# A first load cut at partition 16, and one semaphore for the three sources of a last product (Poisson loss, one core)

## The chip, the cores and the metric

One core of one Trainium2 chip. The metric is device microseconds (us) of the run; a profile's span begins with the first DMA issue and is 1.3 to 1.5 us shorter.

## The reference

```python
def setup_inputs():
    batch, dim = 1024, 4096
    # log_input: randn, target: integers 0..9, both float32

def reference(log_input, target):
    loss = np.exp(log_input) - target * log_input
    return np.mean(loss, axis=-1).astype(np.float32)
```

Two inputs of 16 MiB are read once, and 4 KiB are written.

## The kernel before

Each partition takes eight consecutive rows of each input (128 KiB of it). SyncE issues all loads; ScalarE takes exponentials with row sums, VectorE products with row sums; the last row is cut into small loads, so that little is left to do when the last bytes land. The last product also adds up the partial sums of that row.

```python
    x_v = log_input.rearrange("(p b) d -> p (b d)", b=nb)
    ...
    early = []
    for i, (what, lo, w) in enumerate(loads):
        ...
        src = x_v if what == "x" else t_v
        dma = nc.sync.dma_start(out=place(what, lo, w), in_=src[:, lo : lo + w])
        dma.then_inc(landed[i], 16)
        if lo < 6 * d:
            early.append(dma.ins)
    before_first_barrier(nc, early)      # the first four loads go out ahead of the start barrier
    ...
    for j, (lo, w, i) in enumerate(t_work):
        ...
        nc.vector.wait_ge(landed[x_load], 16)
        if j < n_t - 1:
            ...   # product of (up to) one row: .wait_op(landed[i], 16).then_inc(prod_done, 1)
        else:
            nc.vector.wait_ge(ones_done, 1)
            nc.vector.wait_ge(landed[i], 16)
            nc.vector.wait_ge(prod_done, n_t - 1)
            nc.vector.tensor_tensor_reduce(
                ...   # the last 384 columns and the partial sums of the last row
            ).wait_op(exp_done, n_x, "sem-ge").then_inc(loss_done, 1)
```

Of the kernel before, what the change touches and what calls it, by code (L numbers as in the profile page):

```python
# [8 lines left out]


TAIL = [("x", 24), ("t", 12), ("t", 12), ("x", 6), ("t", 5), ("x", 2), ("t", 3)]


def before_first_barrier(nc, instructions):





    here, first = nc.cur_bb.bb, nc.main_func.blocks[0]  # L20
    names = {i.name for i in instructions}
    here.instructions = [i for i in here.instructions if i.name not in names]
    at = next(
        k
        for k, i in enumerate(first.instructions)
        if i.engine == mybir.EngineType.SP and i.opcode == "Drain"
    )
    first.instructions = first.instructions[:at] + instructions + first.instructions[at:]


def kernel(tc, log_input, target, out):














    nc = tc.nc
    tc.close()
    tc.compile()  # L48

    P = nc.NUM_PARTITIONS  # L50
    n, d = log_input.shape
    nb = n // P
    assert nb * P == n and tuple(target.shape) == (n, d) and nb == 8 and d % 32 == 0
    inv_d = 1.0 / d
    last_row = nb - 1

    x_v = log_input.rearrange("(p b) d -> p (b d)", b=nb)
    t_v = target.rearrange("(p b) d -> p (b d)", b=nb)
    out_v = out.rearrange("(p b) -> p b", b=nb)


    loads = []
    for first, rows in ((0, 4), (4, 2), (6, 1)):
        loads += [("x", first * d, rows * d), ("t", first * d, rows * d)]
    at = {"x": last_row * d, "t": last_row * d}
    for what, w in TAIL:
        loads.append((what, at[what], w * d // 32))
        at[what] += w * d // 32
    assert at == {"x": nb * d, "t": nb * d}


    def work(kind):
        todo = []
        for i, (what, lo, w) in enumerate(loads):
            if what == kind:
                step = min(w, d)
                todo += [(a, step, i) for a in range(lo, lo + w, step)]
        return todo

    x_work, t_work = work("x"), work("t")  # L80
    n_x, n_t = len(x_work), len(t_work)
    n_parts = n_x - last_row + n_t - last_row - 1

    big = {
        "x": nc.alloc_sbuf_tensor("x_big", [P, 4 * d + n_parts], F32).ap(),
        "t": nc.alloc_sbuf_tensor("t_big", [P, 4 * d + n_parts], F32).ap(),
    }
    mid = {
        "x": nc.alloc_sbuf_tensor("x_mid", [P, 2 * d], F32).ap(),
        "t": nc.alloc_sbuf_tensor("t_mid", [P, 2 * d], F32).ap(),  # L90
    }

    def place(what, lo, w):
        row = lo // d
        if 4 <= row < 6:
            return mid[what][:, lo - 4 * d : lo - 4 * d + w]
        if row >= 6:
            lo -= (6 if row == 6 else 4) * d
        return big[what][:, lo : lo + w]

    e_dump = nc.alloc_psum_tensor("e_dump", [P, d], F32).ap()

    parts = nc.alloc_sbuf_tensor("parts", [P, 2 * last_row], F32).ap()
    join_dump = nc.alloc_sbuf_tensor("join_dump", [P, 2 * last_row], F32).ap()
    all_loss = nc.alloc_sbuf_tensor("all_loss", [P, nb], F32).ap()

    def part(k):
        return big["t"][:, 4 * d + k : 4 * d + k + 1]

    landed = [nc.alloc_semaphore(f"landed{i}") for i in range(len(loads))]  # L110
    exp_done = nc.alloc_semaphore("exp_done")
    prod_done = nc.alloc_semaphore("prod_done")
    join_done = nc.alloc_semaphore("join_done")
    ones_done = nc.alloc_semaphore("ones_done")
    loss_done = nc.alloc_semaphore("loss_done")
    out_done = nc.alloc_semaphore("out_done")


    early = []
    for i, (what, lo, w) in enumerate(loads):  # L120
        if what == "x" and lo in (6 * d, 7 * d):
            free = 1 if lo == 6 * d else 4
            nc.sync.wait_ge(exp_done, free)
            nc.sync.wait_ge(prod_done, free)  # L124
        src = x_v if what == "x" else t_v
        dma = nc.sync.dma_start(out=place(what, lo, w), in_=src[:, lo : lo + w])  # L126
        dma.then_inc(landed[i], 16)
        if lo < 6 * d:
            early.append(dma.ins)
    before_first_barrier(nc, early)  # L130


    nc.gpsimd.memset(big["x"][:, 4 * d : 4 * d + n_parts], -1.0).then_inc(ones_done, 1)  # L133


    def join(row, exps):
        nc.scalar.wait_ge(exp_done, exps)
        nc.scalar.activation(  # L138
            out=join_dump[:, 2 * row : 2 * row + 2],
            in_=parts[:, 2 * row : 2 * row + 2],  # L140
            func=ACT_F.Copy,
            scale=inv_d,
            accum_out=all_loss[:, row : row + 1],
        ).wait_op(prod_done, row + 1, "sem-ge").then_inc(join_done, 1)

    for k, (lo, w, i) in enumerate(x_work):
        row, col = lo // d, lo % d
        if col == 0 and row >= 2:
            join(row - 2, k)
        elif col == 0 and row == 1:  # L150
            nc.scalar.wait_ge(exp_done, k)
        nc.scalar.activation(  # L152
            out=e_dump[:, col : col + w],
            in_=place("x", lo, w),
            func=ACT_F.Exp,
            bias=0.0,
            scale=1.0,
            accum_out=parts[:, 2 * row : 2 * row + 1] if row < last_row else part(k - last_row),
        ).wait_op(landed[i], 16, "sem-ge").then_inc(exp_done, 1)
        if col == 0 and row == last_row:  # L160
            join(row - 1, k + 1)


    for j, (lo, w, i) in enumerate(t_work):
        row = lo // d
        x_load = next(ix for a, wx, ix in x_work if a + wx >= lo + w)
        nc.vector.wait_ge(landed[x_load], 16)  # L167
        if j < n_t - 1:
            nc.vector.tensor_tensor_reduce(  # L169
                out=place("t", lo, w),  # L170
                in0=place("t", lo, w),
                in1=place("x", lo, w),
                scale=-1.0,
                scalar=0.0,
                op0=ALU.mult,
                op1=ALU.add,
                accum_out=parts[:, 2 * row + 1 : 2 * row + 2]
                if row < last_row
                else part(n_x - last_row + j - last_row),
            ).wait_op(landed[i], 16, "sem-ge").then_inc(prod_done, 1)  # L180
        else:
            nc.vector.wait_ge(ones_done, 1)
            nc.vector.wait_ge(landed[i], 16)  # L183
            nc.vector.wait_ge(prod_done, n_t - 1)  # L184
            nc.vector.tensor_tensor_reduce(  # L185
                out=place("t", lo, w + n_parts),
                in0=place("t", lo, w + n_parts),
                in1=place("x", lo, w + n_parts),
                scale=-inv_d,
                scalar=0.0,  # L190
                op0=ALU.mult,
                op1=ALU.add,
                accum_out=all_loss[:, last_row : last_row + 1],
            ).wait_op(exp_done, n_x, "sem-ge").then_inc(loss_done, 1)


    nc.sync.wait_ge(join_done, last_row)
    nc.sync.dma_start(out=out_v, in_=all_loss).wait_op(loss_done, 1, "sem-ge").then_inc(
        out_done, 16
    )  # L200
    used = landed + [exp_done, prod_done, join_done, ones_done, loss_done]
    nc.sync.sem_clear(range(used[0].num, out_done.num))
    assert all(used[0].num <= s.num < out_done.num for s in used)
    nc.sync.wait_ge(out_done, 16).then_inc(out_done, -16)
# [30 lines left out]
```

## Time and profile before

| | before |
|---|---|
| time | 84.22 us (84.13 to 84.23) |
| span of the profile | 82.7 us |
| first exponential starts (first load landed) | 21.73 us |
| first product starts (second load landed) | 41.07 us |
| last product starts | 80.67 us |
| store issued | 81.27 us |

The first two loads are 8 MiB each, so their landings give the rate of the stream and the lateness of its start. The lines (start, length, engine, line, output and inputs):

```profile
21.73 3.59 ACT L152 ACTIVATE e_dump<-x_big 128x4096 f32<-128x4096 f32 x1 [17.47 <-DMA x_big<-in_log_input_dram]
41.07 4.43 DVE L169 CUSTOM_DVE_ANT_0 t_big<-t_big,x_big 128x4096 f32<-128x4096 f32 x1 [41.07 <-DMA t_big<-in_target_dram]
```

The lines of the start and of the end are shown in the prediction.

### The profile page before, as it was taken

Reading aid. Unit: us, or ns where it says so; the run is one execution under the profiler, and the core shown is the slowest. Engines: PE = TensorE matmul, PEld = TensorE weight load, DVE = VectorE, ACT = ScalarE, POOL = GpSimd, SP = SyncE. Lnnn points to the kernel's source line nnn. Section 1 sums busy time; section 2 is a strip of 40 time slices with the busy share of each in tenths; the row PEclk is TensorE's granted clock in tenths of the full one; section 3 lists DMA queues with packets and bytes.
Section 4 is the critical chain, followed back from the end, with each engine's and each line's share of the span. In section 5 each row is a group of like instructions: output and inputs, shape, how many; then the busy total and the mean of one; then the engine's idle time right before and its main releaser. Section 6 shows DMA issues by size and latency. Waiting matters only on the chain.

```text
span 82.7 us, 136 instructions
## 1 busy us (share of the span) xinstructions
DVE 35.6 (43%) x22; ACT 33.2 (40%) x35; POOL 0.3 (0%) x5
## 2 busy tenths in 40 slices
DVE  0000000000000000000199999999379995994982
ACT  0500000000499910000000998979792595029360
POOL 0000000000000000000000000000000000000000
DMA  9199999919999991999599699799799999999960
GB/s 507 63 444 507 507 507 507 507 63 444 507 507 507 507 475 63 475 507 507 254 507 475 285 507 507 317 444 507 341 420 404 483 388 436 380 413 428 403 214 2
DMA packets 2016, 33.56 MB, mean 406 GB/s; under 512 B 352, under 2 KB 608, under 8 KB 1120
## 3 DMA queue, kind: packets, MB, share of 16 engines
q1 hardware_dynamic: 2016, 33.56, 95.6%
HBM read 33.55 MB, written 0.00 MB: 406 GB/s over the span
## 4 chain that ended last, share of the span: by engine, by line
DMA 72%; DVE 14%; issue 10%; SPq 2%; DVEq 0%
DMA t_big<-in_target_dram 72%; DVE t_big L169 13%; SPq L126 2%; DVE t_big L185 1%; DVE parts L169 0%; DVEq L184 0%; DVEq L183 0%; DVEq L167 0%; SPq L124 0%; DVE all_loss L185 0%
## 5 line engine op out<-in xcount | busy, mean ns | idle before, releaser
L169 DVE CUSTOM_DVE_ANT_0 t_big<-t_big,x_big 128x4096 f32<-128x4096 f32 (+2 forms) x8 | 26.2, 3308 | 43.4 <-DMA t_big<-in_target_dram 43.2
L152 ACT ACTIVATE e_dump<-x_big 128x4096 f32<-128x4096 f32 (+3 forms) x8 | 21.8, 2730 | 23.9 <-DMA x_big<-in_log_input_dram 23.6
L138 ACT ACTIVATE join_dump<-parts 128x2 f32<-128x2 f32 x7 | 1.4, 203 | 20.4 <-DVE parts L169 20.3
L169 DVE CUSTOM_DVE_ANT_0 t_mid<-t_mid,x_mid 128x4096 f32<-128x4096 f32 x2 | 8.8, 4422 | 2.0 <-DMA t_mid<-in_target_dram 2.0
L152 ACT ACTIVATE e_dump<-x_mid 128x4096 f32<-128x4096 f32 x2 | 7.1, 3568 | 0.0
L152 ACT ACT_TABLE_LOAD x1 | 1.3, 1283 | 3.0 <-PEq L48 3.0
L152 ACT ACTIVATION_READ_ACCUMULATOR e_dump<-x_big 128x1 f32 x8 | 1.5, 186 | 0.0
L138 ACT ACTIVATION_READ_ACCUMULATOR join_dump<-parts 128x1 f32 x7 | 1.3, 187 | 0.0
L185 DVE CUSTOM_DVE_ANT_0 t_big<-t_big,x_big 128x390 f32<-128x390 f32 x1 | 0.6, 568 | 0.2 <-ACT e_dump L152 0.2
L169 DVE DVE_READ_ACCUMULATOR2_ANT parts<- 128x1 f32 x7 | 0.6, 83 | 0.0
L152 ACT ACTIVATION_READ_ACCUMULATOR e_dump<-x_mid 128x1 f32 x2 | 0.4, 186 | 0.0
L169 DVE DVE_READ_ACCUMULATOR2_ANT t_big<- 128x1 f32 x3 | 0.3, 84 | 0.0
L133 POOL MEMSET x_big<- 128x6 f32 x1 | 0.1, 103 | 2.5 <-POOLq L48 2.5
L219 POOL MEMSET const-uint8-127<- 128x1 uint8 x1 | 0.1, 102 | 0.0
L219 POOL MEMSET const-bfloat16-1.0<- 128x1 bf16 x1 | 0.1, 101 | 0.0
L219 POOL MEMSET const-float32-0.0<- 128x1 f32 x1 | 0.1, 98 | 0.2 <-issue 0.2
L219 POOL MEMSET const-float32-1.0<- 128x1 f32 x1 | 0.1, 98 | 0.0
L185 DVE DVE_READ_ACCUMULATOR2_ANT all_loss<- 128x1 f32 x1 | 0.1, 85 | 0.0
## 6 DMA issues: line engine op xcount, KB each, us to landing
x_mid<-in_log_input_dram SPq DMA_DIRECT2D x1, 4096.0 KB, 49.9
t_mid<-in_target_dram SPq DMA_DIRECT2D x1, 4096.0 KB, 59.1
x_big<-in_log_input_dram SPq DMA_DIRECT2D x1, 2048.0 KB, 19.8
t_big<-in_target_dram SPq DMA_DIRECT2D x1, 2048.0 KB, 24.3
x_big<-in_log_input_dram SPq DMA_DIRECT2D x1, 1536.0 KB, 15.3
t_big<-in_target_dram SPq DMA_DIRECT2D x2, 768.0 KB, 17.5
x_big<-in_log_input_dram SPq DMA_DIRECT2D x1, 384.0 KB, 18.7
t_big<-in_target_dram SPq DMA_DIRECT2D x1, 320.0 KB, 19.1
```

Source lines behind the costliest of these rows:

```text
L126: dma = nc.sync.dma_start(out=place(what, lo, w), in_=src[:, lo : lo + w])
L133: nc.gpsimd.memset(big["x"][:, 4 * d : 4 * d + n_parts], -1.0).then_inc(ones_done, 1)
L138: nc.scalar.activation(out=join_dump[:, 2 * row : 2 * row + 2], in_=parts[:, 2 * row : 2 * row + 2], func=ACT_F.Copy, scale=inv_d, accum_o ...
L152: nc.scalar.activation(out=e_dump[:, col : col + w], in_=place("x", lo, w), func=ACT_F.Exp, bias=0.0, scale=1.0, accum_out=parts[:, 2 * ro ...
L169: nc.vector.tensor_tensor_reduce(out=place("t", lo, w), in0=place("t", lo, w), in1=place("x", lo, w), scale=-1.0, scalar=0.0, op0=ALU.mult ...
L185: nc.vector.tensor_tensor_reduce(out=place("t", lo, w + n_parts), in0=place("t", lo, w + n_parts), in1=place("x", lo, w + n_parts), scale= ...
L219: nc = _bacc.Bacc("TRN2", target_bir_lowering=False, num_devices=1)
```

## The change

The intent of the first part: the last product waits for three late sources. Where two of them are awaited by separate wait instructions, those run one after the other once the sources are in (0.05 us each, at 80.44 and 80.54 us in the chain of the kernel before); if all three count on one semaphore, which the product waits on itself, no wait instruction is left between the last source and the product. The intent of the second part: a first load of 16 partitions is one row for each of 16 DMA engines, so that all engines might begin sooner.

```diff
+FIRST = 16
-    landed = [nc.alloc_semaphore(f"landed{i}") for i in range(len(loads))]
+    landed = [nc.alloc_semaphore(f"landed{i}") for i in range(len(loads) - 1)]
+    full = [32] + [16] * (len(loads) - 2)
+    last_ready = nc.alloc_semaphore("last_ready")
...
-        dma = nc.sync.dma_start(out=place(what, lo, w), in_=src[:, lo : lo + w])
-        dma.then_inc(landed[i], 16)
+        cuts = [0, FIRST, P] if i == 0 else [0, P]
+        sem = landed[i] if i < len(loads) - 1 else last_ready
+        for a, b in zip(cuts, cuts[1:]):
+            dma = nc.sync.dma_start(out=place(what, lo, w)[a:b], in_=src[a:b, lo : lo + w])
+            dma.then_inc(sem, 16)
...
-        ).wait_op(landed[i], 16, "sem-ge").then_inc(exp_done, 1)
+        ).wait_op(landed[i], full[i], "sem-ge").then_inc(
+            exp_done if k < n_x - 1 else last_ready, 1
+        )
...
-        nc.vector.wait_ge(landed[x_load], 16)
+        if j == 0 or x_load > t_work[j - 1][2]:
+            nc.vector.wait_ge(landed[x_load], full[x_load])
...
-            ).wait_op(landed[i], 16, "sem-ge").then_inc(prod_done, 1)
+            ).wait_op(landed[i], full[i], "sem-ge").then_inc(
+                prod_done if j < n_t - 2 else last_ready, 1
+            )
         else:
             nc.vector.wait_ge(ones_done, 1)
-            nc.vector.wait_ge(landed[i], 16)
-            nc.vector.wait_ge(prod_done, n_t - 1)
+            nc.vector.wait_ge(exp_done, n_x - 1)
+            nc.vector.wait_ge(prod_done, n_t - 2)
...
-            ).wait_op(exp_done, n_x, "sem-ge").then_inc(loss_done, 1)
+            ).wait_op(last_ready, 18, "sem-ge").then_inc(loss_done, 1)
```

More of the change, by code (lines that the diff above doesn't have):

```diff
@@ L125 @@
         src = x_v if what == "x" else t_v
-        dma = nc.sync.dma_start(out=place(what, lo, w), in_=src[:, lo : lo + w])
-        dma.then_inc(landed[i], 16)
-        if lo < 6 * d:
-            early.append(dma.ins)
+        cuts = [0, FIRST, P] if i == 0 else [0, P]
[3 more added lines that the diff above has]
+            dma.then_inc(sem, 16)
+            if lo < 6 * d:
+                early.append(dma.ins)
     before_first_barrier(nc, early)
@@ L200 @@
     )
-    used = landed + [exp_done, prod_done, join_done, ones_done, loss_done]
+    used = landed + [last_ready, exp_done, prod_done, join_done, ones_done, loss_done]
     nc.sync.sem_clear(range(used[0].num, out_done.num))
```

## The prediction

> **What bounds the kernel now.** I read the page's busy shares and slices first, then the chain of work that ended last, then the timelines of both ends, then the DMA rates over short windows at the start. From the page:
>
> ```profile
> DVE 35.6 (43%) x22; ACT 33.2 (40%) x35; POOL 0.3 (0%) x5
> DMA  9199999919999991999599699799799999999960
> q1 hardware_dynamic: 2016, 33.56, 95.6%
> ```
>
> No engine is half busy; the DMA slices are full from the first to the last but one (a lone 1 is an effect of the record: a large packet is booked where it starts). The queue is busy for 95.6% of 82.7 us. So the kernel is one stream of 33.55 MB, and the span is the time until the stream runs, plus the stream, plus a tail after it. The stream's rate: the timeline starts the first exponential, which waits for the first load, at 21.73 us and the first product, which waits for the second load, at 41.07. Both loads are 8 MiB, so 8 MiB take 19.34 us: 434 GB/s, or 27.1 GB/s for each of 16 engines, and one row of 64 KiB takes an engine 2.42 us. The whole 32 MiB at that rate are 77.4 us of the 82.7. The end, in the chain:
>
> ```profile
> 60.46 19.11 DMA t_big<-in_target_dram
> 79.57 0.02 issue
> 79.60 0.83 DVE t_big L169 x2
> 80.43 0.01 issue
> 80.44 0.05 DVEq L183
> 80.49 0.05 issue
> 80.54 0.05 DVEq L184
> 80.59 0.09 issue
> 80.67 0.57 DVE t_big L185
> 81.24 0.01 DVE all_loss L185
> ```
>
> L183 and L184 are separate wait instructions ahead of the last product (L185); between the end of the previous product (80.43) and the start of the last there are 0.24 us of nothing but waits and their dispatch. The timeline says when the three sources were ready:
>
> ```profile
> 79.95 0.39 ACT L152 ACTIVATE e_dump<-x_big 128x256 f32<-128x256 f32 x1 [0.27 <-DMA x_big<-in_log_input_dram]
> 80.28 0.19 ACT L152 ACTIVATION_READ_ACCUMULATOR e_dump<-x_big 128x1 f32 x1
> 80.35 0.08 DVE L169 DVE_READ_ACCUMULATOR2_ANT t_big<- 128x1 f32 x1
> 80.67 0.57 DVE L185 CUSTOM_DVE_ANT_0 t_big<-t_big,x_big 128x390 f32<-128x390 f32 x1 [0.24 <-ACT e_dump L152]
> 81.27 0.35 SPq L198 DMA_DIRECT2D out_dram<-all_loss  x1
> ```
>
> The last exponential's sum is out at 80.28 + 0.19 = 80.47, the product before at 80.43. The third source, the last load, comes from the view of DMA issues: issued at 61.42 and 19.0 us to landing, so at about 80.42. All three come within 0.06 us of each other. The start, as engine rates in windows of 0.2 to 0.5 us (the last two columns are DMA share and GB/s):
>
> ```profile
> 0.50:1.00 0.50, 0.00 (x0) 0.00 (x0) 0.00 (x0) 1.00 0.39 131
> 1.00:1.20 0.20, 0.00 (x0) 0.00 (x0) 0.00 (x0) 1.00 11.02 3604
> 1.20:1.40 0.20, 0.00 (x0) 0.00 (x0) 0.00 (x0) 1.00 1.92 655
> 1.40:1.60 0.20, 0.00 (x0) 0.00 (x0) 0.00 (x0) 1.00 0.83 328
> 1.80:2.00 0.20, 0.00 (x0) 0.00 (x0) 0.00 (x0) 1.00 0.76 328
> ```
>
> Rate times window is the bytes of the packets that start in it; over 65,536 this gives 1, 11, 2, 1 and 1 packets: sixteen, one for each engine. The first engine starts 1.0 us after the first issue began, the last nearly 1 us later. The trace starts the second packets at 4.05 to 4.44 us; less 2.42 us, the engines are at full rate, in effect, only from 1.63 to 2.03 us on.
>
> [...]
>
> **The change, part by part.** (a) *The last product's waits.* The last load, the next-to-last product and the last exponential now raise one semaphore (16 + 1 + 1 = 18), and the product waits for it itself. What still stands ahead as wait instructions is met early: the exponentials but one by 79.69, the products but two by 79.54, the next-to-last load at 60.94 + 19.0 = 79.94. So those waits finish by about 80.1[...]. From semaphore to start is then one hop, as for the 640-wide product: landing at 79.57, start at 79.60, 0.02 us. New start: 80.47 + 0.02 = 80.49 or 80.50 instead of 80.67. Gain 0.17 us, all of it on the path, as only the product, its accumulator, the store and its landing (80.67 to 82.7) follow.
>
> (b) *Redundant waits.* Five of the products lose a wait for a load that an earlier product has already waited for, about 21 ns each on the sequencer, ahead of the engine: 0.
>
> (c) *One issue more.* SP issues five loads before the barrier in place of four: 0.38 to 0.43 us and a gap of 0.04. The barrier and the table load (2.98 to 4.3 us now) move 0.45 us later; the first exponential needs the table at 21.7: 0. The second issue is out at about 0.8 us, long before the engines are done with their first 64 KiB at about 4 us: no gap in the stream.
>
> (d) *The split's purpose.* [...] The most that can be had is the spread: from 1.63-2.03 down to about 1.0, that is 0.6 to 1.0 us. But fourteen engines had packets by 1.4 us and still reached full rate only at 1.63 or later, so most of that is latency that a smaller load does not remove. I put the gain at 0.1 us, between -0.1 (nothing, and a little lost) and 0.4.
>
> Sum: 84.22 - 0.17 - 0.1 = 83.95; I say 84.0.
>
> **The rivals.** *First rival: the ports.* [...] the first 1 MiB takes 4 x 2.42 = 9.7 us instead of 2.4[...]. [...] the end moves by at least that, to about 93.6. The load of 112 partitions then makes it worse if each engine has seven neighbouring rows: [...] I add up to 7 us as a rough estimate, for about 101. [...] Against: nothing in this trace shows a port as the bound rather than an engine, and if the rows of a small load were dealt to engines as in the full load, engines 0 to 3 would take rows 0 to 15 and the others would go straight on. I can't settle it from here, and give it somewhat less than even chances. [...]
>
> *Second rival: the split starts the stream later.* If the 16 rows go to few engines, the other engines get their first descriptor from the second issue, 0.4 us later: +0.4 - 0.17, about 84.4.
>
> *Third rival: the tail wait is replaced.* The exponential (80.47) ends after both others, and it ends when its load came (79.94) plus 0.53. The combined wait can't be met sooner than that; if dispatch from the queue takes 0.1 us instead of 0.02, part (a) gains 0.1. Engines are far from being the bound at 43%.
>
> **Range and chances.** The outcome has two heaps: 83.5 to 84.4 where the split is harmless (weight 0.55), and 86 to 101 where ports bind (0.45). Faster by over 2% would need 1.7 us, more than the whole spread at the start plus the tail: 0.01. The point stays on the heavier heap, 84.0; a range for 8 in 10 has to reach well into the other: 83.5 to 98.0.
>
> **What would show it.** Right: the last product starts 0.02 to 0.05 us after the last exponential's sum, with no wait instruction between; the first exponential starts at 21.6 to 21.8 us and the first product 19.3 us later. Wrong by the ports: DMA slices near 2 or rates of about 108 GB/s in the first 10 us, the first exponential at 29 us or later, and the same 19.34 us for the second load or more. Wrong at the start: the first exponential at over 22.0 us. Wrong at the tail: the product still 0.2 us behind its last source.

## The result, and the profile after

The changed kernel takes 105.65 us (105.08 to 106.14, six runs), before 84.22: ratio 1.2549, 95% interval 1.2509 to 1.2589. (A ratio is the mean time of one kernel's fast runs over that of the other's of the same rounds, so not quite the ratio of the medians.) It is slower by a quarter.

| | before | after | difference |
|---|---|---|---|
| first exponential starts | 21.73 | 43.80 | +22.07 |
| first product starts | 41.07 | 62.98 | +21.91 |
| from the first to the second landing | 19.34 | 19.18 | -0.16 |
| last product starts | 80.67 | 102.33 | +21.66 |
| span | 82.7 | 104.4 | +21.7 |

```profile
43.80 3.59 ACT L163 ACTIVATE e_dump<-x_big 128x4096 f32<-128x4096 f32 x1 [38.97 <-DMA x_big<-in_log_input_dram]
62.98 4.42 DVE L183 CUSTOM_DVE_ANT_0 t_big<-t_big,x_big 128x4096 f32<-128x4096 f32 x1 [62.98 <-DMA t_big<-in_target_dram]
```

All of the loss is there when the first load has landed; the second 8 MiB, and all that follows, take what they took. The page of the changed kernel:

```profile
DMA  9009190991994949999999999999999999999930
GB/s 402 0 0 377 25 402 0 402 352 50 402 301 100 301 100 352 402 402 402 402 402 402 427 402 440 477 440 402 427 427 389 427 440 427 410 400 426 389 133 2
q1 hardware_dynamic: 2032, 33.56, 95.3%
```

The queue is busy for 95.3% of the span, before 95.6%: the busy share does not see the loss. The record books a packet as busy until it ends, however slowly it moves (8.5 us on average for the first sixteen here, 3.1 before). The rates see the loss. Columns of the next view: window, its length, busy time of VectorE, ScalarE and GpSimd, clock, DMA share, GB/s, for the changed kernel:

```profile
10.00:20.00 10.00, 0.00 (x0) 0.00 (x0) 0.00 (x0) 1.00 0.78 190
30.00:40.00 10.00, 0.00 (x0) 0.00 (x0) 0.00 (x0) 1.00 0.99 229
50.00:60.00 10.00, 0.00 (x0) 1.31 (x2) 0.00 (x0) 1.00 0.98 426
```

While the first load runs, sixteen engines at a share of 0.99 move 229 GB/s; in the second load, at 0.98, they move 426. The end of the chain in the changed kernel answers to the one shown in the prediction:

```profile
101.77 0.05 DVEq L200
101.82 0.39 issue
102.21 0.10 DVE t_big L183
102.31 0.02 issue
102.33 0.57 DVE t_big L201
```

The last wait instruction (L200) is done at 101.82, half a microsecond ahead of the last product (L201), which starts 0.02 us after the sum of the product before it. That part works as predicted.

### The profile page after: what moved, and what is told of

Read it like the earlier page. It is cut to its first block, busy times and chain, and to the rows that moved or that the text cites. A ratio compares the mean times of both kernels' runs of the same rounds, so it can differ in the third digit from the quotient of the medians.

```text
span 104.4 us, 132 instructions
## 1 busy us (share of the span) xinstructions
DVE 35.6 (34%) x22; ACT 33.2 (32%) x35; POOL 0.3 (0%) x5
## 3 DMA queue, kind: packets, MB, share of 16 engines
q1 hardware_dynamic: 2032, 33.56, 95.3%
## 4 chain that ended last, share of the span: by engine, by line
DMA 60%; another core or an unknown queue 18%; DVE 14%; issue 4%; SPq 2%; DVEq 0%
DMA x_big<-in_log_input_dram 60%; DVE t_big L183 14%; SPq L137 2%; DVE t_big L201 1%; DVE parts L183 0%; DVEq L200 0%; DVEq L181 0%; SPq L132 0%; DVE all_loss L201 0%
## 5 line engine op out<-in xcount | busy, mean ns | idle before, releaser
L163 ACT ACTIVATE e_dump<-x_big 128x4096 f32<-128x4096 f32 (+3 forms) x8 | 21.8, 2730 | 45.3 <-DMA x_big<-in_log_input_dram 44.9
L201 DVE CUSTOM_DVE_ANT_0 t_big<-t_big,x_big 128x390 f32<-128x390 f32 x1 | 0.6, 566 | 0.0
L201 DVE DVE_READ_ACCUMULATOR2_ANT all_loss<- 128x1 f32 x1 | 0.1, 82 | 0.0
```

The source lines that it names most:

```text
L163: nc.scalar.activation(out=e_dump[:, col : col + w], in_=place("x", lo, w), func=ACT_F.Exp, bias=0.0, scale=1.0, accum_out=parts[:, 2 * ro ...
L201: nc.vector.tensor_tensor_reduce(out=place("t", lo, w + n_parts), in0=place("t", lo, w + n_parts), in1=place("x", lo, w + n_parts), scale= ...
```

## The experiments

Two theories of the loss. *Places*: engines that write to some destination partitions at the same time hold each other up; what counts is which partitions one load reaches. *The split itself*: two loads on one semaphore, a small load ahead of a large one, few rows for each engine, or the source rows in HBM that are read together.

**Each part alone, and a cut of the other kind.** The first kernel has the semaphores without the split, the second the split without the semaphores, the third cuts the first load by columns.

```diff
 e1_sem_only, against the changed kernel
-        cuts = [0, FIRST, P] if i == 0 else [0, P]
+        cuts = [0, P]                      # and full = [16] * (len(loads) - 1)
 e2_split_only, against the kernel before
+        cuts = [0, 16, P] if i == 0 else [0, P]      # landed[0] is waited for at 32
 e3_columns, against the changed kernel
+        cuts = [0, w // 8, w] if i == 0 else [0, w]
-            ... out=place(what, lo, w)[a:b], in_=src[a:b, lo : lo + w])
+            ... out=place(what, lo, w)[:, a:b], in_=src[:, lo + a : lo + b])
```

> The semaphore part alone, first load whole. In the changed kernel's trace the last product starts 0.02 us after its last source, where it was 0.20 us in the kernel before. If that gain is real time, this kernel takes 84.22 - 0.17 = 84.05 us, ratio 0.998, and the last product starts at about 80.50 us. If the gain is a shift in the trace only (or the part costs something elsewhere), the ratio is 1.000 or above.

> The split of the first load alone, all waits of the last product as before. If the whole loss is the split's: 105.65 + 0.17 = 105.8 us, the first exponential at about 43.8 us. If the loss came from the two parts together or from the semaphores: near 84.2.

> The change as it is, but the first load is cut by columns (the first eighth of each of 128 rows, then the rest): again two loads of 1 and 7 MiB on one semaphore and one issue more, but both reach all partitions. Theory of places (only few SBUF partitions in one load is what costs): as without a split, 84.05 us, first exponential at 21.7 to 22.0 us. Rival, that a second load on one semaphore or a small load ahead of a large one breaks up the stream: well over 90 us.

| | time | ratio to before (95%) | first exponential |
|---|---|---|---|
| e1_sem_only | 84.04 | 0.9982 (0.9969 to 0.9995) | 21.91 |
| e2_split_only | 105.87 | 1.2591 (1.2546 to 1.2636) | 43.59 |
| e3_columns | 83.99 | 0.9974 (0.9959 to 0.9989) | 21.92 |

The split alone is the whole loss, and the semaphores alone are a small gain: 0.18% of 84.2 us is 0.15 us, and the interval leaves out zero. The cut by columns has the same bytes in both loads, the same two counts on one semaphore and the same extra issue, and costs nothing that can be told from e1. So neither the split as such nor the small first load does it. The chain of e1 shows the gain's place:

```profile
80.13 0.52 ACT e_dump L163 x2
80.65 0.02 issue
80.67 0.57 DVE t_big L201
```

The product starts 0.02 us after the last exponential's sum; in the kernel before it was 0.20 us. (In this profile the stream began to run some 0.18 us later, as the 21.91 says, so the product stands at the same 80.67.)

**Loads by themselves.** A kernel issues twelve loads of 64 KiB rows into one buffer, each waited for before the next; its output is zeros (m2 and m3 below too).

```diff
 m1_places: all work of the kernel before is replaced by
+    nc.sync.dma_start(out=x_big[0:128], in_=x[0:128, 0:w]).then_inc(s[0], 16)
+    nc.sync.wait_ge(s[0], 16)
+    nc.sync.dma_start(out=x_big[0:16], in_=x[0:16, 0:w]).then_inc(s[1], 16)
+    nc.sync.wait_ge(s[1], 16)
+    ...    # and ten more, on the partitions of the table
```

> Twelve loads of 64 KiB rows, one after the other, each waited for; the result is zeros on purpose. From issue to landing, by destination partitions (and source rows). Theory of ports [...]: 128: 21.7; 0-15 from rows 0-15: 12; 0-15 from every eighth row: 12 as well; every eighth partition from rows 0-15[...]: 7; 16-31 from rows 0-15: 12; 0-3: 12; 0,4,8,12 from rows 0-3: 4.6; 0-31: 12; 0-63: 21.6; 16-127: 29 to 36; 0-111: the same; 128 again: 21.7. Rival, the source rows in HBM (neighbouring rows read at once are slow): 0-15 from every eighth row drops to about 5, every eighth partition from rows 0-15 stays at 12, and 0,4,8,12 from rows 0-3 equals 0-3. Rival, that small loads run on few engines: 0-31 takes 12, but 0,4,8,12 equals 0-3.

The timeline of SyncE: the start of one issue to the start of the next is one load from issue to landing.

```profile
1.38 0.38 SPq L91 DMA_DIRECT2D x_big<-in_log_input_dram  x1
23.28 0.35 SPq L93 DMA_DIRECT2D x_big<-in_log_input_dram  x1
34.87 0.31 SPq L95 DMA_DIRECT2D x_big<-in_log_input_dram  x1
46.65 0.57 SPq L97 DMA_DIRECT2D x_big<-in_log_input_dram  x1
54.09 0.32 SPq L99 DMA_DIRECT2D x_big<-in_log_input_dram  x1
65.95 0.30 SPq L101 DMA_DIRECT2D x_big<-in_log_input_dram  x1
76.83 0.66 SPq L103 DMA_DIRECT2D x_big<-in_log_input_dram  x1
81.72 0.34 SPq L105 DMA_DIRECT2D x_big<-in_log_input_dram  x1
94.23 0.53 SPq L107 DMA_DIRECT2D x_big<-in_log_input_dram  x1
117.00 0.32 SPq L109 DMA_DIRECT2D x_big<-in_log_input_dram  x1
150.14 0.31 SPq L111 DMA_DIRECT2D x_big<-in_log_input_dram  x1
183.16 0.35 SPq L113 DMA_DIRECT2D x_big<-in_log_input_dram  x1
204.98 0.37 SPq L115 DMA_DIRECT2D out_dram<-all_loss  x1
```

| line | partitions | source rows | us to landing | expected | one packet (64 KiB), us |
|---|---|---|---|---|---|
| L91 | 0-127 | 0-127 | 21.9 | 21.7 | 2.42 (the first 2.8 to 3.4) |
| L93 | 0-15 | 0-15 | 11.6 | 12 | 7.9 to 9.3 |
| L95 | 0-15 | every eighth | 11.8 | 12 | 7.7 to 9.0 |
| L97 | every eighth (16) | 0-15 | 7.4 | 7 | 4.2 to 5.5 |
| L99 | 16-31 | 0-15 | 11.9 | 12 | 7.8 to 9.2 |
| L101 | 0-3 | 0-3 | 10.9 | 12 | 7.9 to 8.2 |
| L103 | 0,4,8,12 | 0-3 | 4.9 | 4.6 | 2.6 to 3.1 |
| L105 | 0-31 | 0-31 | 12.5 | 12 | 5.1 (second row) |
| L107 | 0-63 | 0-63 | 22.8 | 21.6 | 5.1 (second to fourth row) |
| L109 | 16-127 | 16-127 | 33.1 | 29 to 36 | 2.7 to 5.6, mostly 4.4 |
| L111 | 0-111 | 0-111 | 33.0 | 29 to 36 | 3.1 to 5.1, mostly 4.6 |
| L113 | 0-127 | 0-127 | 21.8 | 21.7 | 2.42 |

(The expected times are the author's estimate: for 0,4,8,12 one packet of 2.42 us, for 0-15 four in turn, and some 2.2 us besides, where the kernel before has 21.73 - 8 x 2.42 = 2.4 us; how many go in turn was assumed. The last column is from the trace's record of each packet.) That column must be read with care. Landing comes 1.8 us after the end of the last packet's record for L101, 0.3 us for L103, so the lengths may understate the cost of a crowded destination; the time to landing does not. The trace also has each increment of a load's semaphore: sixteen for L93, at 10.7 to 11.6 us after the issue, four for the four rows of L101 beside an early one at 0.4. This fits one engine for each row.

L101 and L103 are the cleanest pair: the same source rows, the same bytes and four packets each, and only the destination partitions differ: 10.9 us against 4.9. L93 and L95 have the same destination and different source rows: no difference. So the source rows are not the cause, and the places are. And 112 rows take 11 us longer than 128.

**Halves.** One number of the change is altered:

```diff
-FIRST = 16
+FIRST = 64
```

> The change with the first load cut at partition 64 in place of 16. Ports: [...] the load of 0-63 measured alone had packets of 5.12 us where 2.42 are normal; eight rows for each engine then take 41 us in place of 19.3, the first exponential comes at about 43.5 us, and the time is 84.05 + 21.6 = 105.7 us. If it is the smallness of the first load that costs: between 84 and 95. If the halves ran beside each other: 84.1.

105.4 us, ratio 1.2515 (1.2497 to 1.2534), first exponential at 43.32 us: 0.3 us and 0.2 us from what was worked out from L107. Its rate while the first load runs, in the view used above:

```profile
10.00:20.00 10.00, 0.00 (x0) 0.00 (x0) 0.00 (x0) 1.00 1.02 210
```

Loads to one half of the partitions run at 210 GB/s where a load to all 128 runs at 434. No load is small here, and the loss is the same.

**Why 112 rows are slow throughout.** Most packets of L109 and L111 take 4.4 to 4.6 us, where those of L113 take 2.42. If only a few engines were in each other's way at a time, most packets should stay at 2.4 us. They don't. Two more kernels of loads put one row on each engine, on partitions chosen so that, as assumed, no, one, two or more pairs of engines are in each other's way (`x_big[28:89:4]` for 28,32,..,88, and so on). Of single partitions the loads show only that 0 and 1 hold each other up (4.4 to 4.7 us) and 0 and 4 do not (3.3 to 3.5); for the larger loads they show how many packets are slow.

```diff
 m2_collide and m3_pairs, against m1_places: other partitions, for instance
+    nc.sync.dma_start(out=x_big[11:117:7], in_=x[0:16, 0:w]).then_inc(s[1], 16)   # no pair
+    nc.sync.dma_start(out=x_big[28:89:4], in_=x[0:16, 0:w]).then_inc(s[2], 16)    # one pair
+    nc.sync.dma_start(out=x_big[24:85:4], in_=x[0:16, 0:w]).then_inc(s[3], 16)    # two pairs
```

> Thirteen more loads of 64 KiB rows, each waited for (zeros on purpose). First 128 rows as a reference. Then 16 rows, one for each engine, on partitions [...] (11,18,..,116); with one pair of engines on one port (28,32,..,88); two pairs (24,28,..,84); four pairs (31,34,..,76); eight pairs (0,8,..,120). If only the engines that meet are slowed: in every load with a pair its longest packets take about 4.8 us and the others 2.4 to 3; the median packet stays at 2.9 for one, two and four pairs. If a shared port also holds up engines that go elsewhere: the median packet rises already at two pairs towards 4.4, as in the load of 112. Then 8 rows on 8 ports, with one pair, with four pairs: 2.6 to 3; then 4.8 for two of eight; then 4.8 for all. Two rows on one port 4.4 to 4.9, two rows on two ports 2.6 to 2.9, one row 2.6 to 2.9. 0 to 95 (six rows for each engine): if as bad as 112, 6 x 4.3 + 2.3 = 28 us; with engines slowed only where they meet about 24.

> Why the 112 rows cost 33 us[...]: in the load before, two pairs of engines at two ports held up all sixteen, one pair only itself. Packets by load, 64 KiB each, one row for each engine. One pair again (36,40,..,96; 3,10,..,108; 28,32,..,88): two packets above 4.1 us, fourteen near 3. Two pairs again (40,..,100; 0,7,..,105; 24,..,84): if two shared ports hold up everybody, all sixteen at 4.2 to 5.3. The load 24,..,84 from every eighth source row: the same if it is the destination, near 3 if it is the source. Two pairs with eight rows on each half of the partitions (24,29,..,99): all slow if it is the two shared ports; only four slow if what counted was that ten engines write to one half. Fewer engines: 24,..,68 (twelve engines, two pairs), 0,3,..,21 (eight engines, two pairs): all slow, or only the four that meet. 24,..,52[...]: all near 3. 2,4,6,8 (one pair of four): two slow.

Packets by load, from the trace's record of each packet, with the pairs assumed; where two groups of lengths are clearly apart, both are given:

```
engines  pairs* partitions           packets, us     (* assumed)
16       0      11,18,..,116         16 of 2.6-3.3
16       1      28,32,..,88          14 of 2.5-3.3, 2 of 4.2-4.5
16       1      28,32,..,88 (m3)     14 of 2.4-3.2, 2 of 4.0-4.3
16       1      36,40,..,96          14 of 2.4-3.3, 2 of 4.3-4.7
16       1      3,10,..,108          14 of 2.4-3.2, 2 of 4.3-4.6
16       2      24,28,..,84          16 of 4.3-5.2 (again in m3: 4.4-5.2)
16       2      the same, source every eighth row: 16 of 4.0-5.2
16       2      40,44,..,100         16 of 4.1-4.8
16       2      0,7,..,105           16 of 3.9-5.0
16       2      24,29,..,99 (8+8)    16 of 4.1-5.2
16       4      31,34,..,76          16 of 4.3-5.3
16       8      0,8,..,120           16 of 4.1-5.3
12       2      24,28,..,68          12 of 3.8-5.0
 8       0      0,4,..,28            8 of 2.6-3.3
 8       0      24,28,..,52          8 of 2.7-3.2
 8       1      3,6,..,24            6 of 2.4-3.1, 2 of 4.0-4.4
 8       2      0,3,..,21            8 of 4.2-5.0
 8       4      0,2,..,14            8 of 3.8-5.1
 4       1      2,4,6,8              2 of 3.3, 2 of 4.3-4.6
 2       1      0,1                  2 of 4.4-4.7
 2       0      0,4                  2 of 3.3-3.5
```

The same can be read without the packets: in a window that holds one load of one row for each engine, DMA share times length is the mean packet. From m3 (columns as above, with GpSimd alone): one pair, two pairs, one pair again, two pairs with eight rows on each half.

```profile
23.28:30.27 6.99, 0.00 (x0) 1.00 0.45 150
30.27:37.38 7.11, 0.00 (x0) 1.00 0.62 147
85.96:92.56 6.60, 0.00 (x0) 1.00 0.46 159
99.89:107.50 7.61, 0.00 (x0) 1.00 0.62 138
```

0.45 x 6.99 = 3.1 us and 0.46 x 6.60 = 3.0 us with one pair; 0.62 x 7.11 = 4.4 us and 0.62 x 7.61 = 4.7 us with two. If only four engines were slowed, as two pairs would have it, the mean would be (12 x 3.0 + 4 x 4.5) / 16 = 3.4 us, an estimate from the lengths in the table. The increments of the semaphores, a second record in the trace, agree. Of sixteen engines with one pair, fourteen are counted 4.6 to 5.1 us after the issue and two at 6.4 to 7.0; with two pairs all sixteen at 6.2 to 7.5.

So the loads fall into three kinds. With no assumed pair no packet took over 3.5 us (four loads); with one, two packets took 4.0 to 4.7 us and the others 3.3 at most (seven loads); with two or more every packet took 3.8 to 5.3 us (eleven loads, eight of them with exactly two). One partition less at one end and one more at the other is enough: 28,..,88 has two slow packets, 24,..,84 sixteen. And 24,..,52 has no slow packet, where 24,..,68, with four partitions more, has twelve of twelve. It isn't ten engines on one half (24,29,..,99 has eight on each) and not the source rows (every eighth row gives the same). What in the chip holds the engines up, no run shows. (A miss beside it: a single row took 3.3 us and two rows on partitions 0 and 4 3.3 to 3.5, where 2.6 to 2.9 had been expected; why is open.)

The last load of m2, partitions 0-95, took 32.3 us, slower than both readings of the expectation (28 and 24). After the first row its packets take 4.8 to 5.1 us throughout, so that sixteen engines on 96 partitions also run at half rate (2.42 us with 128).

**More waits, for the other part.** The kernel before with one wait more ahead of the last product:

```diff
             nc.vector.wait_ge(prod_done, n_t - 1)
+            nc.vector.wait_ge(exp_done, n_x)
```

> The kernel before with one more wait of VectorE for the exponentials ahead of the last product. If wait instructions that come after the last source cost what the trace shows (0.05 us each and 0.05 between them), the product starts 0.30 us after its last source in place of 0.20, and the time is 84.3 us. If the gain of the semaphore part came from something else (the order in which sources are counted): no change, 84.2.

84.27 us, ratio 1.0005 (0.9991 to 1.0019): not to be told from before. In the profile the product starts 0.26 us after the last exponential's sum, not 0.30: three wait instructions end up there, the first of 0.02 us, and they run partly before that source is in. The traces show the step: 0.02 to 0.03 us in the four kernels with the new semaphores (the changed one, e1, e3, e4), about 0.20 in the two without (before, e2), 0.26 here. The time of this run alone does not show it.

## Why the prediction was wrong

**The point stood on the wrong heap.** The step that failed is the judgement that a first load of 16 partitions does no harm: it got a weight of 0.55, and 84.0 was put there. The first rival, that engines hold each other up when they write to partitions 0 to 15, is what happened (packets of 7.5 to 9.3 us, where a load of 128 rows has 2.42); it had 0.45, and whether a port is what they share was not shown. Two arguments stood against it. That nothing in the trace showed such a bound was true, but the trace had no such load. The other, that "if the rows of a small load were dealt to engines as in the full load, engines 0 to 3 would take rows 0 to 15 and the others would go straight on", fails. In the changed kernel the first sixteen packets start at 1.0 to 1.7 us and take 7.5 to 9.3 us side by side, as those of L93 do (7.9 to 9.3); four engines with four rows each would have taken them in turn. That a trace shows no such bound should have weighed little where it had no such load.

**The rival's size was short as well.** It said about 93.6 from the first load and "up to 7 us" more for the 112 rows, about 101; the range ended at 98.0 and the measured 105.65 is outside. The first term was about right: the packets of the first 1 MiB averaged 8.5 us in the changed kernel, and it had landed by 11.9 us, where 9.7 us of writing were expected (four packets of 2.42 us in turn; the four was assumed). The second was mis-sized: 112 rows alone take 33.1 us to landing, 128 rows 21.9, so 11.2 us and not up to 7. With 11.2 the rival's own sum is 83.95 + 9.7 + 11.2, about 104.9, near the measured 105.65. The prediction gave no working for its 7 us. The loads of m2 and m3 show that rows on sixteen partitions four apart can slow all sixteen engines (24,..,84: sixteen packets of 4.3 to 5.2 us). The trace of the 112 rows shows most rows slow and few fast: of the packets of L109, the third row's (2.7 to 3.4 us but for two of 4.6) is the fast one, and in L111, where all lies sixteen partitions lower, it is the fourth's. (The row after it lies between, at 3.5 to 3.9 us for most packets.) The changed kernel shows the same: its seven rows after the first 1 MiB average 5.4, 4.8, 3.2, 3.7, 4.5, 4.7 and 4.6 us, and the third and fourth are again the fast ones. That each engine takes seven neighbouring rows was an assumption; the records do not show it for each engine.

**The signs.** Of those named for the first rival, the first exponential after 29 us and an unchanged second load came true. "DMA slices near 2 or rates of about 108 GB/s in the first 10 us" (a quarter of the measured 434; the quarter was assumed) did not: the queue is busy for 95.3% of the span, as said with the page above, and the record has 184 GB/s in the first 10 us, as it books a packet where it starts (4260 GB/s in the window from 1.0 to 1.2 us).

**Part (a), the waits: right.** Predicted 0.17 us; the gap fell from 0.20 to 0.02 us in the profile, and e1 gained 0.15 us in time.

**Part (b) and (c), fewer redundant waits and one issue more: right.** e3 has the extra issue and is not slower than e1. Part (b) was not run apart from (a); in the kernel before, the last wait of L167 takes 0.021 us at 78.8 us, while the product before it is on the engine until 79.5.

**Part (d), an earlier start: the gain isn't there.** Predicted 0.1 us. From the start of the issue, the first packets of the sixteen-row loads L93, L95 and L99 begin at 0.95 to 2.25 us, those of the 128-row loads L91 and L113 at 0.98 to 1.70. In the kernels themselves the first sixteen begin at 1.00 to 1.71 us after the change, 1.00 to 1.92 before, and 0.99 to 1.51 in e1, which has no split. Fewer rows for each engine do not start the engines sooner.

**Second rival, few engines: wrong**, as the first load has sixteen packets side by side. **Third rival, the tail wait replaced: wrong**, the product starts 0.02 us after its last source.

Of these runs the semaphore part without the split by partitions beats both: 84.04 us alone (e1), 83.99 with the cut by columns (e3), not to be told apart.

## What to carry to other kernels

A load's destination partitions decide how fast its DMA engines write (four rows to 0-3 took 10.9 us, the same four to 0,4,8,12 took 4.9): cut a load by columns, over all 128 partitions (83.99 us here), and not by partitions (105.87 us with the cut at 16, 105.4 us at 64), even if it stays on sixteen engines. (Shown here for rows of 64 KiB, issued by SyncE.) A DMA busy share near 1 is no proof of full rate (0.99 at 229 GB/s, 0.98 at 426): look at GB/s, and at the landings of loads of known size. Where several late sources meet, let them count on one semaphore that the consumer waits on itself; here it was worth some 0.15 us, once, at the end of the path.
